# A down projection by seven block products instead of eight, in a two-block transformer kernel

## The chip, the cores and the metric

The kernel runs on one core of a Trainium2 chip. The metric is the device time of one execution in microseconds, taken as the median of several runs. All data are float32, one batch of 1024 tokens with 1024 features.

## The reference, cut to what matters

Two blocks follow each other. The first is attention and a convolutional feed-forward layer, each with a residual and a layer norm:

```
x = layer_norm(ALPHA * x + token_mixer(x), ln1)
u = x @ w_up                       # 1024 -> 2 * 2816
u = causal convolution of width 3 over the tokens, + conv_b
g = value * gelu(gate)             # 1024 tokens x 2816
x = layer_norm(ALPHA * x + g @ w_down, ln2)
```

The second block modulates its activations with six vectors `mod = split(silu(c) @ ada_w + ada_b, 6)`, runs a gated linear attention in two directions (with a context of 256 tokens scanned ahead of the tokens) and a feed-forward layer:

```
a = rmsnorm(x) * (1 + mod[1]) + mod[0]
x = x + mod[2] * gla(a)
h = rmsnorm(x) * (1 + mod[4]) + mod[3]
x = x + mod[5] * (relu(h @ w1) ** 2) @ w2
out = rmsnorm(x)
```

The change concerns `g @ w_down` and the time at which `mod[2]` and `mod[5]` are computed.

## The kernel before, in words

Every float32 operand of a product is split in a high part `h` (cast on ScalarE, L102) and a low part `l` (subtraction on VectorE, L103), and a product is three matmuls, `ah bh + ah bl + al bh` (`mm3`, L130 to L132). A matmul is at most 128 x 128 stationary against 512 moving columns.

The program is written as stages: attention, output projection, first up projection with convolution and gate, first down projection, linear attention, its output projection, second up projection, second down projection. Where stages overlap, `merge` takes generators in turn by the share of a planned cost that each has used. From the order written the framework makes, when it builds the kernel, one fixed order of instructions for each engine: an earlier written instruction goes first among those that are ready by its own estimate of time. A tile takes a free buffer of its tag, and waits if there is none. Loads go out on SyncE's queue (SP), some stores on GpSimd's (POOL), both in order.

The two up projections (`up_pass`) and the second down projection (`mlp_down`) already cut their operands in 2 x 2 blocks and take 7 block products instead of 8, with sums of blocks: left sums S1 to S4, right sums T1 to T4. For the second down projection the left sums are formed in `relu2` and the right ones in `sum_weights`, both stored to device memory and read back as operands.

The first down projection (`ffn_down`) goes a plain way: the gate's result is stored per chunk of 128 hidden features to `g1d` (L1083), and `down_group` takes groups of 2 or 3 chunks, for each group all 8 token tiles and both halves of 512 output columns. `evac` copies (L1111) or adds (L1113) each group's accumulator to `res[t]`; with group 3 it adds the residual, with the last group it forms the layer norm's sum (L585) and calls `layer_norm`. Behind it `norm1(t)` makes the next stage's operands `hi`, `lo`, and `first_values` multiplies them with the first head's value weights. The accumulators have three banks.

Beside the groups run `context` and `modulation`, which calls `ada` for the vectors v = 2 and v = 5, each in four units of 256 columns. A unit loads eight 128 x 256 pieces of `ada_w` (L150), accumulates them on VectorE (L154, L160) in the tile `acc`, of which there is one, and sums over partitions by a matmul (L164). In `ffn_down` the pieces have two buffers of their own (`ar`). The vectors v = 4 and v = 3 are computed in the linear attention, where `ar` is None and the pieces take the four `raw` buffers of `w_get`, through which all weights of that stage pass (L121).

The linear attention writes for each head h: `scan(h)`, then `prepare(h + 1)` (query and key products `fp`, value products `tokp`), then 18 steps of the modulation, which are two units. After the four heads follow the gate products `gate_out` (also `tokp`).

## Time and profile before

| | us |
|---|---|
| median of 3 runs | 2528.82 (2527.7 to 2532.9) |
| profiled execution | 2526.01 |
| its span, first to last instruction | 2524.3 |
| mean granted TensorE clock | 0.992 |

The profile is of one execution. Durations of an engine's groups are unions of its instructions' times, with the mean of one behind them in ns. Matmuls are pipelined, so that the next one starts before the one before it has ended; a stretch of time divided by the matmuls in it gives their spacing. PEclk is the granted TensorE clock as a share of 2.4 GHz.

### The profile page before, as it was taken

How to read it: one execution, taken by the hardware profiler on the slowest of the kernel's cores; microseconds unless marked ns; L12 is line 12 of the kernel's file. 1: busy time of each engine (PE TensorE's matmuls, PEld its weight loads, DVE VectorE, ACT ScalarE, POOL GpSimd, SP SyncE). 2: the span in 40 equal slices, each digit the busy share in tenths (PEclk: the TensorE clock that was granted, in tenths of full speed). 3: DMA queues.
4: the chain of work that ended last, by engine and by line, in shares of the span. 5: the costliest groups of instructions: out<-in, count | busy, mean ns of one | idle time of the engine just before them, and what ended most of it. 6: DMA issues, size and time to landing. Idle time of an engine off the chain costs nothing. (4 is left out here: it accounts for less than half of the span.)

```text
span 2524.3 us, 36732 instructions
## 1 busy us (share of the span) xinstructions
PE 2448.2 (97%) x12954; PEld 2079.2 (82%) x12954; DVE 1707.5 (68%) x3207; ACT 1226.6 (49%) x2208; POOL 416.7 (17%) x655
## 2 busy tenths in 40 slices
PE   8999999998999999899999999999999999999998
PEld 7898989777788888788878798899788888778886
DVE  5776666758777777688658866643588767455456
ACT  5555555734555454653216643332355545544443
POOL 4576641520000000000004000000111111100000
PEclk9999999998999999999999999999999999999999
DMA  5333231253222221465332121211526776566565
GB/s 176 93 92 105 85 87 57 89 186 116 84 76 80 79 90 69 152 195 189 121 119 99 50 71 63 64 61 34 180 94 242 295 272 243 211 234 213 194 209 192
DMA packets 164793, 338.18 MB, mean 134 GB/s; under 512 B 19832, under 2 KB 52216, under 8 KB 164608
## 3 DMA queue, kind: packets, MB, share of 16 engines
q1 hardware_dynamic: 146208, 269.76, 32.8%
q0 software_dynamic: 18400, 66.07, 7.0%
q8 instruction: 102, 1.67, 0.3%
q14 instruction: 83, 0.68, 0.1%
HBM read 247.12 MB, written 80.25 MB: 130 GB/s over the span
## 5 line engine op out<-in xcount | busy, mean ns | idle before, releaser
L130 PE MATMUL s<-act_hi,uh 128*128 128x512 f32 (+1 forms) x640 | 247.2, 386 | 2.0 <-ACT res L774 2.0
L132 PE MATMUL s<-act_hi,ul 128*128 128x512 f32 (+1 forms) x640 | 246.6, 385 | 0.0
L131 PE MATMUL s<-act_lo,uh 128*128 128x512 f32 (+1 forms) x640 | 246.5, 385 | 0.0
L103 DVE TENSOR_TENSOR dpart<-draw,dpart 128x512 fp32r<-128x512 f32 x224 | 146.0, 688 | 124.8 <-ACT dpart L102 123.4
L568 POOL TENSOR_TENSOR rstd<-rstd,mhalf 128x1 f32<-128x1 f32 x74 | 52.6, 713 | 939.8 <-DVE rstd L567 903.2
L102 ACT CAST dpart<-draw 128x512 fp32r<-128x512 f32 x224 | 129.7, 620 | 150.9 <-PE Y L131 66.2
L130 PE MATMUL down<-wdh,gh 128*128 128x512 f32 x352 | 141.6, 403 | 10.9 <-ACT res L1111 5.6
L130 PE MATMUL tokp<-wh,act_hi 128*128 128x256 f32 (+1 forms) x512 | 149.0, 293 | 1.1 <-ACT wh L102 1.1
L132 PE MATMUL tokp<-wh,act_lo 128*128 128x256 f32 (+1 forms) x512 | 148.4, 291 | 1.4 <-DVE act_lo L103 1.4
L131 PE MATMUL tokp<-wl,act_hi 128*128 128x256 f32 (+1 forms) x512 | 149.1, 293 | 0.0
L130 PEld LDWEIGHTS s<-act_hi,uh 128*128 128x128 f32 x640 | 121.7, 190 | 28.4 <-ACT res L774 2.7
L131 PEld LDWEIGHTS s<-act_lo,uh 128*128 128x128 f32 x640 | 121.7, 190 | 25.6
L132 PEld LDWEIGHTS s<-act_hi,ul 128*128 128x128 f32 x640 | 121.5, 190 | 25.8
L131 PE MATMUL down<-wdl,gh 128*128 128x512 f32 x352 | 138.4, 394 | 0.0
L132 PE MATMUL down<-wdh,gl 128*128 128x512 f32 x352 | 136.6, 394 | 0.1
L368 ACT ACTIVATE P<-P,mx 128x640 f32<-128x640 f32 (+7 forms) x128 | 94.4, 738 | 85.7 <-DVE mx L365 79.5
L370 POOL TENSOR_SCALAR P<-P,mx 128x640 f32<-128x640 f32 (+7 forms) x128 | 95.2, 747 | 192.4 <-DVE mx L369 158.5
L130 PE MATMUL s<-ext_8hi,uh 128*128 128x512 f32 (+1 forms) x320 | 123.1, 385 | 0.0
L131 PE MATMUL s<-ext_8lo,uh 128*128 128x512 f32 (+1 forms) x320 | 123.1, 385 | 0.0
L132 PE MATMUL s<-ext_8hi,ul 128*128 128x512 f32 (+1 forms) x320 | 122.9, 384 | 0.0
L103 DVE TENSOR_TENSOR ul<-res,uh 128x1024 fp32r<-128x1024 f32 x80 | 96.6, 1209 | 31.7 <-ACT uh L102 31.3
L102 ACT CAST uh<-s 128x512 fp32r<-128x512 f32 (+1 forms) x72 | 60.3, 837 | 104.8 <-PE s L131 103.2
(364 smaller groups left out, 7275.7 us busy)
## 6 DMA issues: line engine op xcount, KB each, us to landing
ada_w<-in_ada_w SPq DMA_DIRECT2D x192, 128.0 KB, 2.2
res<-in_w_up SPq DMA_DIRECT2D x44, 512.0 KB, 3.4
res<-in_mlp_w SPq DMA_DIRECT2D x32, 512.0 KB, 4.3
draw<-in_mlp_w SPq DMA_DIRECT2D x48, 256.0 KB, 3.4
g1d<-res POOLq DMA_DIRECT2D x22, 512.0 KB, 2.9
gload<-g1d SPq DMA_DIRECT2D x22, 512.0 KB, 4.6
wdraw<-in_w_down SPq DMA_DIRECT2D x44, 256.0 KB, 3.3
raw<-in_wqk SPq DMA_DIRECT2D x32, 256.0 KB, 3.1
```

The source lines that it names most:

```text
L102: ACT.copy(h, raw)
L103: DVE.tensor_tensor(out=l, in0=raw, in1=h, op=ALU.subtract)
L130: PE.matmul(out=o, lhsT=ah, rhs=bh, start=first, stop=False, **kw)
L131: PE.matmul(out=o, lhsT=ah, rhs=bl, start=False, stop=False, **kw)
L132: return PE.matmul(out=o, lhsT=al, rhs=bh, start=False, stop=last, **kw)
L368: ACT.activation(Pm[:, 0:W], Pm[:, 0:W], AF.Exp, bias=mx[:, 0:1], scale=-1.0, accum_out=mx[:, 1:2])
L370: POOL.tensor_scalar(out=Pm[:, 0:W], in0=Pm[:, 0:W], scalar1=mx[:, 2:3], scalar2=0.0, op0=ALU.mult, op1=ALU.add)
L568: POOL.tensor_tensor(out=t[:, 1:2], in0=t[:, 0:1], in1=mhalf, op=ALU.pow)
```

## The change

The first down projection takes 7 block products over all of K: the 22 chunks are 11 pairs (even chunk, odd chunk), tokens and output columns are cut in halves of 512. The right sums (T1 to T4) of `w_down` are formed in the attention by `right_sums` and stored; the left sums are formed in `conv_gate` by `left_sums` for each pair and stored instead of `g1d`. `ffn_down` reads all operands back, product by product, 4 accumulators at a time in five banks; the transposes (`xtp`) share the banks of the context's products. `down_group` is gone. The modulation vectors 2 and 5 are computed in the linear attention, with 36 steps behind each head, in the order 2, 4, 3, 5.

```diff
+    def right_sums(W, n, pl, dst, load, store):
+        w, v = (pl.tile([P, D], F32, tag=x, name=f"sum{x}") for x in "wv")
+        for i, t in enumerate((w, v)):
+            load.dma_start(out=t.rearrange("p (h c) -> p h c", h=2), in_=W[2 * n + i].rearrange("h p c -> p h c"))
+        yield 1
+        DVE.tensor_tensor(out=w[:, XS], in0=w[:, YS], in1=w[:, XS], op=ALU.subtract)
+        DVE.tensor_tensor(out=w[:, YS], in0=v[:, YS], in1=w[:, YS], op=ALU.subtract)
+        yield 1
+        DVE.tensor_tensor(out=v[:, YS], in0=v[:, YS], in1=w[:, XS], op=ALU.subtract)
+        DVE.tensor_tensor(out=v[:, XS], in0=v[:, XS], in1=v[:, YS], op=ALU.subtract)
+        yield 1
+        for x, t in zip(dst, (w, v)):
+            store.dma_start(out=x[n], in_=t)
+    def left_sums(ga, gb, a, b):
+        DVE.tensor_tensor(out=a[:, XS], in0=ga[:, YS], in1=gb[:, YS], op=ALU.add)
+        DVE.tensor_tensor(out=a[:, YS], in0=a[:, XS], in1=ga[:, XS], op=ALU.subtract)
+        DVE.tensor_tensor(out=ga[:, YS], in0=ga[:, XS], in1=ga[:, YS], op=ALU.subtract)
+        DVE.tensor_tensor(out=b, in0=gb[:, XS], in1=a[:, YS], op=ALU.subtract)
...
+        twp = pool(st, "tw", 1)
...
+        def down_sums():
+            for n in range(NCH // 2):
+                yield from right_sums(I["w_down"], n, twp, TW, SP, SP)
+        tws = down_sums()
...
-            merge([(some(mod, 13), 13), (until_pair(), attn_cost(p)), (feed[0], ...), (split_ys(p), 6)])
+            merge([(some(mod, 13), 13), (some(tws, 5), 5), (until_pair(), attn_cost(p)), (feed[0], ...), (split_ys(p), 6)])
...
+        if n % 2 == 0:
+            even[:] = [convc[1].tile([P, T], F32, tag="g", name="geven")]
+            DVE.tensor_tensor(out=even[0], in0=o[0], in1=o[1], op=ALU.mult)
+            return
         DVE.tensor_tensor(out=o[0], in0=o[0], in1=o[1], op=ALU.mult)
-        POOL.dma_start(out=g1d[n], in_=o[0])
+        a, b = convc[1].tile([P, D], F32, tag="s12", name="sums12"), convc[1].tile([P, 512], F32, tag="s4", name="sums4")
+        left_sums(even[0], o[0], a, b)
+        for x, t in (("A12A22", o[0]), ("A11S3", even[0]), ("S1S2", a)):
+            POOL.dma_start(out=left1[x][n // 2], in_=t)
+        POOL.dma_start(out=narrow1["S4"][n // 2], in_=b)
...
+    def block_product(B, raw, left, right, pairs, psums, a, b, by_tile, mm):
+        def operand(name, n, pl, tag):
+            r = raw.tile([P, 512], F32, tag="raw", name="draw")
+            SP.dma_start(out=r, in_=B[name](n))
+            pl = pl()
+            h, l = (pl.tile([P, 512], F32R, tag=tag + x, name="dpart") for x in "hl")
+            split(r, h, l)
+            return h, l
+        def some(t, n, ab):
+            (ah, al), (bh, bl) = ab
+            mm(psums[t], ah[:, toks(t)], al[:, toks(t)], bh, bl, n == 0, n == pairs - 1)
+        ops = {}
+        for n in range(pairs):
+            ops[n] = operand(a, n, left, "s"), operand(b, n, right, "t")
+            if n < pairs - by_tile:
+                for t in range(4):
+                    some(t, n, ops[n])
+                yield
+        for t in range(4):
+            for n in range(pairs - by_tile, pairs):
+                some(t, n, ops[n])
+            yield t
...
-        set_banks(st, "f", {"mm": (1, 3, "down"), "c": (1, 2, "z hps fp tokp"), "ct": (1, 1, "ctp ktp dS"), "tp": (1, 2, "xtp ada")}, ...)
+        set_banks(st, "f", {"mm": (1, 5, "down"), "c": (1, 2, "z hps fp tokp xtp"), "ct": (1, 1, "ctp ktp dS xtp")}, ...)
+        counts = ("r0", 2), ("l0", 2), ("draw1", 4), ("l1", 4), ("r1", 4), ("rp", 2), ("fc1", 1)
...
+        def p1(t, p):
+            ACT.copy(res[t][:, XS], p)
+        def p6(t, p):
+            add(res[t + 4][:, XS], p, res[t][:, XS])
+            with_x1(t, XS, res[t][:, XS])
+        def p2(t, p):
+            complete(t, XS, p)
+        def p5(t, p):
+            add(res[t + 4][:, YS], p, res[t + 4][:, XS])
+            with_x1(t, YS, res[t + 4][:, YS])
+            with_x1(t + 4, YS, res[t + 4][:, YS])
+        def p3(t, p):
+            complete(t, YS, p)
+            with_x1(t + 4, XS, res[t + 4][:, XS])
+            normed(t)
+        def p7(t, p):
+            complete(t + 4, YS, p)
+            add(res[t + 4][:, XS], p, res[t + 4][:, XS])
+        def p4(t, p):
+            complete(t + 4, XS, p)
+            normed(t + 4)
...
+            for a, b, f in (("A11", "B11", p1), ("S2", "T2", p6), ("A12", "B21", p2), ("S1", "T1", p5), ("S4", "B22", p3), ("S3", "T3", p7)):
+                for t in run(a, b, f, 3):
...
-        merge([(most(), 207024), (context(cst), CTXSHARE), (modulation(), 72)])
+        merge([(most(), 179784), (context(cst), CTXSHARE)])
...
-        for t in down_group(groups[last], g1d, Wd, pools, evac(last), True):
-            if t >= 1:
-                norm1(t - 1)
-        norm1(NT - 1)
+        ready = deque(range(4))
+        for t in run("A22", "T4", p4, 3):
+            if ready:
+                norm1(ready.popleft())
+        for t in range(4, NT):
+            norm1(t)
...
     def modulation():
-        for v in (4, 3):
+        for v in (2, 4, 3, 5):
...
-        for _ in range(18):
+        for _ in range(36):
             next(mod, None)
```

`with_x1` loads a piece of the block's input and adds ALPHA times it to an operand; `complete` adds an accumulator and forms the sum of the row; `normed` is `layer_norm` and a store.

## Rows read from the trace of the kernel before

**Rows 1.** The page's first part: busy time, share of the span and instructions of each engine, of the whole execution.

```profile
PE 2448.2 (97%) x12954; PEld 2079.2 (82%) x12954; DVE 1707.5 (68%) x3207; ACT 1226.6 (49%) x2208; POOL 416.7 (17%) x655
```

**Rows 2.** Busy time by stretch. Columns: stretch, its length, busy us of PE, PEld, DVE, ACT and POOL with their instructions, granted clock, DMA share, GB/s. In order: attention; first up projection; first down projection with context; its end; linear attention; second down projection.

```profile
0.00:505.00 505.00, 489.14 (x3189) 433.48 (x3189) 347.45 (x920) 300.63 (x665) 264.14 (x416) 1.00 0.33 98
605.00:1045.00 440.00, 431.09 (x1916) 351.05 (x1915) 328.18 (x359) 219.61 (x274) 12.61 (x23) 0.98 0.22 80
1052.00:1364.00 312.00, 301.13 (x1465) 251.35 (x1466) 229.19 (x449) 121.55 (x230) 22.27 (x23) 0.99 0.49 158
1332.00:1372.00 40.00, 40.00 (x219) 34.26 (x218) 36.04 (x85) 22.42 (x43) 20.57 (x19) 1.00 0.22 81
1410.00:1705.00 295.00, 287.54 (x1807) 259.20 (x1806) 186.54 (x480) 122.01 (x286) 16.94 (x29) 1.00 0.19 61
2202.00:2524.00 322.00, 307.65 (x1347) 253.54 (x1345) 183.96 (x300) 146.95 (x268) 8.42 (x12) 0.98 0.62 207
```

**Rows 3.** Groups of TensorE's instructions, shapes kept apart: line, operation, tiles, shape, count, busy us and mean ns of one, then the idle time before them and what ended it. The first down projection, and two rows of the second.

```profile
L130 PE MATMUL down<-wdh,gh 128*128 128x512 f32 x352 | 141.6, 403 | 10.9 <-ACT res L1111 5.6 <-DVE res L1113 3.3 <-ACT wdh L102 1.2
L130 PE MATMUL X<-dpart 128*128 128x512 f32 x256 | 100.2, 391 | 2.4 <-ACT dpart L102 2.4
L131 PE MATMUL X<-dpart 128*128 128x512 f32 x256 | 100.6, 393 | 1.6 <-DVE dpart L103 1.6
```

**Rows 4.** TensorE alone in a steady stretch of the second down projection: stretch, length, busy us, matmuls that touch it, clock, DMA share, GB/s.

```profile
2260.00:2300.00 40.00, 40.00 (x179) 1.00 0.55 184
```

**Rows 5.** Groups of VectorE's and ScalarE's instructions in 1045 to 1364, columns as in rows 3.

```profile
L1113 DVE TENSOR_TENSOR res<-res,down 128x512 f32<-128x512 f32 x96 | 64.5, 682 | 38.4 <-PE down L132 38.1
L103 DVE TENSOR_TENSOR wdl<-wdraw,wdh 128x512 fp32r<-128x512 f32 x44 | 29.9, 685 | 8.4 <-ACT wdh L102 8.4
L160 DVE SCALAR_TENSOR_TENSOR ada_acc<-ada_w,cs,ada_acc 128x256 f32<-128x256 f32 x56 | 26.8, 479 | 18.3 <-DMA ada_w<-in_ada_w 17.9
L103 DVE TENSOR_TENSOR gl<-gload,gh 128x1024 fp32r<-128x1024 f32 x22 | 26.8, 1220 | 6.1 <-ACT gh L102 6.0
...
L102 ACT CAST wdh<-wdraw 128x512 fp32r<-128x512 f32 x44 | 27.3, 623 | 56.9 <-PE down L132 30.8 <-DMA wdraw<-in_w_down 19.3 <-DVE res L1113 6.5
L102 ACT CAST gh<-gload 128x1024 fp32r<-128x1024 f32 x22 | 22.9, 1051 | 35.1 <-PE down L131 29.2 <-DMA gload<-g1d 5.9
```

**Rows 6.** DMA issues of the whole execution: tiles, queue, count, KB each, median us from issue to landing.

```profile
wdraw<-in_w_down SPq DMA_DIRECT2D x44, 256.0 KB, 3.3
...
draw<-A11S3d SPq DMA_DIRECT2D x32, 256.0 KB, 2.9
```

**Rows 7.** What SyncE's queue waited for, of the whole execution: us in total, times, longest. L1390 is the operand load of the second down projection.

```profile
SPq L1390 <- DVE dpart L103: 176.5, 192, 4.5
```

**Rows 8.** The modulation's wide matmuls, of the whole execution: duration in ns (least, median, most), first and last start, shape.

```profile
L164 PE MATMUL ada<-ada_acc,ones x16: 377/378/382, 1084.2 to 1288.4; 128*128 128x256 f32 x16
```

**Rows 9.** SyncE's queue in order of time in 1440 to 1500 and in 1600 to 1650: start, length of the merged row, line, tiles, count.

```profile
1444.04 21.14 SPq L150 DMA_DIRECT2D ada_w<-in_ada_w  x16
1465.46 2.52 SPq L121 DMA_DIRECT2D raw<-in_g_qk  x4
...
1611.42 30.48 SPq L150 DMA_DIRECT2D ada_w<-in_ada_w  x13
1642.36 7.88 SPq L121 DMA_DIRECT2D raw<-in_g_r  x8
```

**Rows 10.** TensorE in order of time, at seven places: start, length, line, tiles, shape, count, and in brackets the idle time before it and what ended it.

```profile
1263.57 0.65 PE L130 MATMUL down<-wdh,gh 128*128 128x512 f32 x1 [2.38 <-DVE res L1113]
...
1364.36 0.30 PE L130 MATMUL tokp<-wh,act_hi 128*128 128x288 f32 x1
...
1461.71 0.28 PE L175 MATMUL ada<-ones,ada_acc 128*128 128x1 f32 x2
...
1493.27 0.50 PE L175 MATMUL ada<-ones,ada_acc 128*128 128x1 f32 x4
...
1494.33 0.40 PE L130 MATMUL fp<-act_hi,wh 128*128 128x512 f32 x1
...
1638.52 0.50 PE L175 MATMUL ada<-ones,ada_acc 128*128 128x1 f32 x4
...
1644.37 0.54 PE L175 MATMUL ada<-ones,ada_acc 128*128 128x1 f32 x4
1646.06 0.50 PE L130 MATMUL tokp<-wh,act_hi 128*128 128x256 f32 x2 [1.15 <-ACT wh L102]
```

**Rows 11.** TensorE in 1646 to 1714, the matmuls of the tile `o` alone and of the tile `dS` alone: stretch, length, busy us, count, clock, DMA share, GB/s.

```profile
1646.00:1714.00 68.00, 14.16 (x59) 1.00 0.13 40
...
1646.00:1714.00 68.00, 8.32 (x28) 1.00 0.13 40
```

**Rows 12.** Two neighbouring stretches behind the wait of 1263.57, columns as in rows 2.

```profile
1263.80:1267.20 3.40, 3.40 (x9) 2.63 (x9) 1.30 (x3) 0.00 (x0) 0.00 (x0) 0.50 0.86 298
1267.20:1270.60 3.40, 3.40 (x17) 2.77 (x16) 1.78 (x3) 0.00 (x0) 0.00 (x0) 1.00 0.14 48
```

**Rows 13.** One of the sum passes of the second up projection (`relu2`), columns as in rows 3.

```profile
L1344 DVE TENSOR_TENSOR sums<-res,sums 128x512 f32<-128x512 f32 x15 | 10.2, 683 | 0.0
```

136 lines of the change are left out of this document (45 added, 91 removed).

## The prediction, made before the change was run

> **What bounds the kernel now.** I read the page's busy shares first: TensorE 97%, VectorE 68%, ScalarE 49% [rows 1]. Then the busy time by stage: the attention (to 505 us), the first up projection (605 to 1045), the first down projection with the context beside it (1052 to 1364), the linear attention (1410 to 1705) and the last product (from 2202) all keep TensorE over 95% busy, so each matmul taken out of a stage shortens it, and each wait put in lengthens it [rows 2]. VectorE is next: 57% to 75% by stage, 90% at the end of the down projection, 1332 to 1372. Third, the waits inside the down projection: 10.9 us, most of them for accumulators not yet copied out (ScalarE's L1111, VectorE's L1113); the last product, which already works with seven block products, waits 2.4 + 1.6 us in all [rows 3].
>
> **Matmuls removed.** Before: 22 chunks x 8 token tiles x 2 halves x 3 = 1056 matmuls of 512 columns. After: 7 products x 11 pairs x 4 tiles x 3 = 924, so 132 go. Their price isn't their duration: the 391 to 403 ns of a row overlap the next matmul. In a steady stretch of the last product 179 matmuls touch 40 us, two of them begun before it: 40 / 177 = 0.226 us each [rows 4]. 132 x 0.226 = **29.8 us** saved. (By the durations it would be 52 us, which counts the overlap twice.)
>
> **Waits of the down projection.** The eight groups of two or three chunks hand TensorE a new accumulator every 1.4 to 2 us with three banks, and 5.6 + 3.3 us are waits for them [rows 3]. After, a product has four accumulators for some 30 us and a fifth bank; only its last three pairs are done tile by tile, 9 matmuls or 2.0 us apart, and a copy takes 0.6 to 0.7 us [rows 5]. I take the waits of the last product, 4.0 us, for the 10.9: **-6.9**; ends 0 and -10.9.
>
> **Operands of the down projection.** Splits before: 22 of 1024 columns and 44 of 512. After: 154 of 512. ScalarE: 154 x 0.623 = 96 us for 50; VectorE: 154 x 0.685 = 105 us for 57, but 64.5 us of L1113 become about 44 passes of 0.69, 30 us, and 27 us of modulation leave [rows 5]. VectorE's 229 of 312 us [rows 2] hardly moves. Loads: 154 x 256 KB = 40 MB for 23, less 8.4 MB of modulation. Four landing buffers turn: 2.9 us from issue to landing [rows 6], 0.62 cast, 0.69 subtraction, some 0.6 of queueing: 4.8 us, 1.2 us an operand. The stage shrinks to about 312 - 42 = 270 us, 1.75 us an operand. So TensorE stays the pace, as in the last product, where the load queue waits 176.5 us for buffers to come free [rows 7] at 1.44 us an operand. Cost nothing; if each turn took 8 us instead (rival 4), the cover would be gone.
>
> **Modulation moved.** Eight units (v = 2 and 5) of eight 128 KB loads, eight VectorE passes and one wide matmul go from the down projection to the linear attention. TensorE's part (16 instructions of at most 0.38 us [rows 8]) is the same in both places: 0. In the down projection they had two load buffers of their own; in the linear attention they share the four `raw` buffers with the weights that TensorE needs. The SyncE rows show the queue: 16 modulation loads take 1444 to 1465, and only behind them come the four loads of the next head's query and key weights (1465.5); at the end the gate weights come at 1642.4, behind the last modulation load [rows 9]. A unit also holds the one accumulator tile until its own small matmul, which TensorE does late: the second unit's at 1493.3, one us ahead of the next head's first product (1494.3). The last two units stand 1638.5 and 1644.4, so a unit takes 5.85 us when TensorE lets it through, and the gate product starts 1.7 us behind [rows 10]. Now four units per head stand there instead of two. Head 0: two more behind 1493.3: 1493.3 + 11.7 + 1.7 = 1506.7, 12.4 us late. Head 1: one of its units can be done between query/key and value products, so one exposed: 6.5 us. Heads 2 and 3 have no weights to load between them but the gate's: four more units, 23.4 us late. Sum 42.3 us. Queued behind: every weight load, then TensorE. What fills it are the scans, which need no weights: in 1646 to 1714 TensorE has 14.2 + 8.3 us of them for `o` and `dS` alone [rows 11], and they are a chain of VectorE and ScalarE, which the 27 us of added VectorE work slows. No row shows how fast a scan runs alone; lower end 0 idle (all filled), upper 42.3 (none). I take two thirds filled, **+15**, nearer the lower, since scan work of about 22 us a head lies beside each delay.
>
> **The clock.** After the 2.38 us wait that ended at 1263.57 [rows 10] the granted clock is 0.50, the 1.2 GHz level, and 9 matmuls touch 3.4 us where the next 3.4 us, at 1.00, hold 17: 8 lost, 1.8 us [rows 12]. The down projection has two such falls, both behind accumulator waits; I take one for the new one, and two in the linear attention: **+1.7**. The Trainium skill (TensorE: Matmul & The Clock Gate, Part 1: The HAM clock gate) says that half rate is the default and activity lifts it; the trace agrees (0.50 behind the 2.38 us wait). By that rule each of the three delays in the linear attention brings a fall, and the sum would be 1.8 us more.
>
> **Sums.** Weight sums: 11 x 4 passes of 0.683 us [rows 13], 30 us of VectorE in the attention, where it is busy 347 of 505 us, and 23 MB more through SyncE. The loads of a pair wait for the stores of the pair before (one buffer each), and bias and weight loads queue behind them. No row shows that: from 0 to a quarter of the passes, 7.5; I take **+2**, since TensorE waits 16 us in the whole stage and part of that is the start. Product sums: 30 us in the up projection, VectorE from 328 to 358 of 440 us (81%), from 0 to 7.5: **+1.5**. The stores, 1.75 MB a pair for 1 MB, go out through GpSimd, busy 13 us there: 0.
>
> **The end of the stage.** Before, eight tiles are normed in the last group; after, four are normed under the last product and four behind it. 36 us of VectorE in 1332 to 1372 for about six tiles [rows 2] is 6 us a tile, 24 us for four, begun 6 us before the product ends; TensorE has 25 us of value products meanwhile. Cost 0 (rival 5 otherwise).
>
> **Sum.** The profiled execution took 2526.0 us: 2526.0 - 29.8 - 6.9 + 15 + 1.7 + 2 + 1.5 = 2509.5. The median of the three runs is 2.8 above the profiled one; some of that I keep: **2511**.
>
> **Rivals.** (1) *Forecast*: as above, 2500 to 2522; chance 0.45. (2) *The modulation hides*: the order of instructions lets units through earlier and scans fill the rest. For it: at 1461.7 a unit's matmul went in the midst of value products; against: the second waited to 1493.3. No idle, no falls there: 2511 - 15 - 3.6 = 2492; 0.25. (3) *The modulation starves the linear attention*: scans don't fill and the whole 42.3 us stand, with one fall more: 2511 + 27.3 + 1.8 = 2540, slower. It decides from about 32 us of idle on, where 29.8 + 6.9 less 5.2 is used up. Against: 22 us of scan work per head; 0.10. (4) *Loads pace the new down projection*, the change failing of its aim: a turn of 8 us makes 154 x 2.0 = 308 us for 270: 2549; TensorE binds up to 1.75 us an operand, each 0.1 beyond costs 15. Against: the last product's 1.44; for: there it has six landing buffers and no context; 0.07. (5) *Banks shared at the end*: the transposes of the norm now use the banks of the value products. If these are handed out in the order written, value products, which start at 1364.36, right behind the last matmul of the stage, while later tiles are still transposed [rows 10], must wait for the seventh tile, about 12 us behind the product's end, with 5 us of transposes in it: +7, 2518; 0.13.
>
> **Range and chances.** 3 and 4 lie above 2530 and hold 0.17; so the range is 2490 to 2527, from the case of no idle to the forecast's with most of it. Within 0.2% of 2528.8 (2523.7 to 2533.9), about what this measurement tells from no change, lie the top of 1 and 5 and a little of 3 and 4: 0.07. Faster 0.80, slower 0.13. With most on one side, the likeliest case's own range is 2500 to 2522.
>
> **What would show it.** In the profile after: 924 matmuls of the down product at a spacing of 0.226; its waits near 4 us, none for an evacuation over 1 us; the stage near 270 us. In the linear attention: 128 modulation loads, the next heads' query and key weights 10 us and 6 us later after the value products than now, a gate product some 20 us later against its scan, TensorE's idle up from 7.5 to some 20 us in that stage, and one or two stretches of clock 0.50. Attention and up projection longer by 1 to 3 us each. I am wrong if the linear attention has no more idle than now (then 2), if it stands for all of its delay (3), if the down projection waits for ScalarE's or VectorE's halves of operands all along it (4), or if value products begin 7 us or more after the last down matmul (5).

## The result and the profile after

The changed kernel takes **2559.8 us** (median of 4 runs, 2552.8 to 2560.5) where the kernel before takes 2529.0 in the same comparison: 1.0113 of it, 95% interval 1.0092 to 1.0134. It is slower; forecast was 2511, with a range to 2527. The profiled execution took 2559.2 us, its span is 2557.5.

The page's first part, as in [rows 1], now of the changed kernel:

```profile
PE 2425.3 (95%) x12822; PEld 2066.3 (81%) x12822; DVE 1744.9 (68%) x3299; ACT 1260.3 (49%) x2284; POOL 445.6 (17%) x677
```

TensorE has its 132 matmuls less and is busy 23 us less, in a span that is 33 us longer: it stands still more. Where, the next table tells. A stage begins with its first matmul; "to the last gate product" begins with the last matmul of the down projection and holds the value products and the linear attention. Us, from the trace of one execution each. The same code scatters from trace to trace: the attention is the same in the changed kernel, e1, e2, e4, e7, e13 and e15 to e18, and takes 523.4 to 528.1 there; the down projection without the modulation takes 283.3 to 290.4, the second up pass with the changed kernel's code 312.8 to 319.8, and the stretch to the last gate product 415.2 to 419.8 in e7, e9, e12 and e18. So a difference of less than some 5 us between two rows means little.

| kernel | attention | first up pass | down projection | to the last gate product | second up pass |
|---|---|---|---|---|---|
| before | 505.4 | 441.6 | 311.4 | 396.0 | 320.9 |
| changed | 525.7 | 430.6 | 287.0 | 446.2 | 315.2 |
| e1 modulation back | 523.4 | 430.6 | 299.9 | 411.0 | 314.9 |
| e2 own load buffers | 524.0 | 430.7 | 283.3 | 419.9 | 317.4 |
| e3 late sums | 528.1 | 430.0 | 286.5 | 447.9 | 317.7 |
| e4 values between norms | 524.5 | 432.0 | 287.0 | 445.9 | 315.5 |
| e5 before, moved 128 bytes | 506.4 | 432.3 | 310.9 | 396.2 | 318.5 |
| e6 sums, transfers only | 513.5 | 431.4 | 285.9 | 445.2 | 315.7 |
| e7 = e2 + own banks | 527.4 | 431.9 | 283.6 | 416.5 | 312.8 |
| e8 sums in up pass | 506.6 | 466.6 | 283.7 | 446.8 | 314.4 |
| e9 = e7, sums on GpSimd in up pass | 507.0 | 465.0 | 287.3 | 419.8 | 315.3 |
| e10 = e9 + modulation on GpSimd | 504.7 | 463.1 | 290.4 | 436.0 | 316.5 |
| e11 = e10 + aligned weights | 513.1 | 462.8 | 289.9 | 430.6 | 315.8 |
| e12 = e7 + paced sums | 532.9 | 429.4 | 287.1 | 415.2 | 317.7 |
| e13 = e7, no passes | 528.1 | 430.8 | 288.4 | 419.0 | 316.5 |
| e14 = e1 + own banks, paced sums | 536.9 | 431.7 | 304.3 | 403.2 | 316.9 |
| e15 = e7, one load | 523.4 | 429.5 | 285.5 | 409.6 | 316.3 |
| e16 = e7, no matmul | 523.9 | 431.9 | 285.6 | 410.7 | 319.8 |
| e17 stores on GpSimd's queue | 524.0 | 433.2 | 286.3 | 446.1 | 317.6 |
| e18 = e7 + e17 | 524.4 | 431.0 | 283.7 | 416.5 | 316.7 |

So the attention loses 20.3, the down projection gains 24.4, the linear attention with the stage's end loses 50.2, and, unforeseen, the two up passes gain 11.0 and 5.7 (the second of these lies within the scatter); with 2.8 lost in the output projection the sum is +32, against 33.2 between the spans.

**The down projection.** TensorE's groups in 1060 to 1356, columns as in [rows 3]:

```profile
L131 PE MATMUL down<-dpart 128*128 128x512 f32 x308 | 121.7, 396 | 0.4 <-DVE dpart L103 0.2
L132 PE MATMUL down<-dpart 128*128 128x512 f32 x308 | 120.9, 393 | 0.0
L130 PE MATMUL down<-dpart 128*128 128x512 f32 x308 | 117.7, 395 | 2.2 <-ACT dpart L102 2.2
```

924 matmuls, and 2.6 us of waits for 10.9 [rows 3]: that part did as forecast. But TensorE's waits in 1065 to 1351 have a new head, the context that runs beside it:

```profile
PE ctp L91 <- ACT ctx_x L943: 4.8, 2, 3.1
PE ctp L91 <- ACT ctx_f L639: 4.2, 1, 4.2
```

Us in all, times, longest. In the kernel before, no wait for the context's norm is among TensorE's in this stage; here it is 9.0 us. Why it was hidden before, no run tells. It is at the stage's start that TensorE stands more, and the granted clock is lower there too. The first 60 us of the stage, changed and before (columns as in [rows 2]):

```profile
1066.00:1126.00 60.00, 49.29 (x219) 39.25 (x219) 38.04 (x59) 39.72 (x77) 6.83 (x10) 0.89 0.82 267
```

```profile
1053.00:1113.00 60.00, 54.41 (x259) 44.62 (x258) 47.94 (x81) 42.69 (x82) 4.76 (x7) 0.97 0.78 265
```

**The end of the stage.** TensorE in order of time; the last down product, the four late norms, the first value product:

```profile
1351.86 0.39 PE L132 MATMUL down<-dpart 128*128 128x512 f32 x1
1363.87 4.46 PE L693 MATMUL xtp<-diag,res 128*128 128x128 f32 x24 [11.62 <-DVE rstd L600]
...
1374.10 0.38 PE L130 MATMUL tokp<-wh,act_hi 128*128 128x288 f32 x1
```

The number in brackets is the engine's idle time before the instruction, and what ended it: 11.6 us of standstill, and the first value product 22.2 us behind the last down product; before it came 0.3 us behind [rows 10]. Of the clock: in 1363.9 to 1367.3, right behind the wait, the granted clock is 0.55, then 1.00.

```profile
1363.90:1367.30 3.40, 3.40 (x17) 3.40 (x18) 3.40 (x5) 1.26 (x3) 2.30 (x3) 0.55 0.21 83
1367.30:1370.70 3.40, 2.05 (x18) 1.86 (x18) 2.62 (x7) 3.40 (x10) 2.00 (x2) 1.00 0.58 228
```

**The linear attention.** SyncE's queue, columns as in [rows 9]: behind the units that are written after head 0, where head 2's weights come next, and the gate weights:

```profile
1465.57 0.85 SPq L150 DMA_DIRECT2D ada_w<-in_ada_w  x2
1491.95 0.33 SPq L169 DMA_DIRECT2D m2d<-ada_o  x1
...
1504.64 3.51 SPq L121 DMA_DIRECT2D raw<-in_g_qk  x4
...
1699.94 4.79 SPq L121 DMA_DIRECT2D raw<-in_g_r  x5
```

For 26 us, 1466 to 1492, nothing leaves, because the queue's head, the store of a unit, waits for VectorE's work on a unit, as SyncE's waits in 1455 to 1495 show (us in all, times, longest):

```profile
SPq L169 <- DVE ada_acc L154: 26.2, 2, 25.7
```

Head 2's weights go out at 1504.6, before at 1465.5 [rows 9]; the gate's at 1699.9, before at 1642.4. TensorE shows what they wait for: units of modulation that come to their matmul only at 1490.7 and later, head 2's first product right behind the last:

```profile
1490.66 0.59 PE L164 MATMUL ada<-ada_acc,ones 128*128 128x256 f32 x2
1498.89 0.59 PE L164 MATMUL ada<-ada_acc,ones 128*128 128x256 f32 x2
1507.91 0.64 PE L164 MATMUL ada<-ada_acc,ones 128*128 128x256 f32 x2
1508.79 0.50 PE L130 MATMUL fp<-act_hi,wh 128*128 128x512 f32 x1
...
1703.23 1.22 PE L164 MATMUL ada<-ada_acc,ones 128*128 128x256 f32 x2 [3.00 <-DVE ada_acc L160]
1703.89 0.99 PE L130 MATMUL tokp<-wh,act_hi 128*128 128x256 f32 x2
```

Then all 768 gate matmuls stand in one block without a break, while the last scan ran alone before them. The same 58 us in the changed kernel and before (columns as in [rows 2]):

```profile
1646.00:1704.00 58.00, 40.46 (x197) 30.43 (x196) 37.64 (x106) 14.47 (x40) 5.87 (x10) 0.89 0.41 126
```

```profile
1646.00:1704.00 58.00, 57.94 (x427) 55.77 (x427) 24.92 (x64) 20.46 (x53) 4.72 (x8) 1.00 0.14 46
```

### The profile page after: what moved, and what is told of

It reads as the page before. It is cut to its first block, busy times and chain, and to the rows that moved or that the text cites. A ratio compares the mean times of both kernels' runs of the same rounds, so it can differ in the third digit from the quotient of the medians.

```text
span 2557.5 us, 37112 instructions
## 1 busy us (share of the span) xinstructions
PE 2425.3 (95%) x12822; PEld 2066.3 (81%) x12822; DVE 1744.9 (68%) x3299; ACT 1260.3 (49%) x2284; POOL 445.6 (17%) x677
## 5 line engine op out<-in xcount | busy, mean ns | idle before, releaser
L103 DVE TENSOR_TENSOR dpart<-draw,dpart 128x512 fp32r<-128x512 f32 x378 | 250.6, 693 | 183.2 <-ACT dpart L102 175.9
L102 ACT CAST dpart<-draw 128x512 fp32r<-128x512 f32 x378 | 221.5, 620 | 243.5 <-PE Y L131 65.7
L131 PEld LDWEIGHTS s<-act_lo,uh 128*128 128x128 f32 x640 | 121.7, 190 | 22.2
L131 PE MATMUL down<-dpart 128*128 128x512 f32 x308 | 121.7, 396 | 0.4 <-DVE dpart L103 0.2
L132 PE MATMUL down<-dpart 128*128 128x512 f32 x308 | 120.9, 393 | 0.0
L102 ACT CAST uh<-res 128x1024 fp32r<-128x1024 f32 x80 | 83.0, 1040 | 77.0 <-PE s L131 61.4
L130 PE MATMUL down<-dpart 128*128 128x512 f32 x308 | 117.7, 395 | 2.2 <-ACT dpart L102 2.2
```

What stands on the lines that cost most here:

```text
L102: ACT.copy(h, raw)
L103: DVE.tensor_tensor(out=l, in0=raw, in1=h, op=ALU.subtract)
L130: PE.matmul(out=o, lhsT=ah, rhs=bh, start=first, stop=False, **kw)
L131: PE.matmul(out=o, lhsT=ah, rhs=bl, start=False, stop=False, **kw)
L132: return PE.matmul(out=o, lhsT=al, rhs=bh, start=False, stop=last, **kw)
```

## The experiments

The diffs show only the lines that matter; a remark behind `#` in them isn't in the kernel. Ratios are to the kernel before, with a 95% interval behind them.

### What starves the linear attention

**e1**: the modulation back beside the down projection.

```diff
+        merge([(most(), 179784), (context(cst), CTXSHARE), (modulation(), 72)])   # v = 2, 5; own ar (2), ac (1); "ada" on bank "c"
-        for _ in range(36):
+        for _ in range(18):                                                       # linear attention: v = 4, 3
```

> The changed kernel, with the modulation v = 2 and 5 put back beside the down projection (two load buffers of its own, 8 units there; 18 steps per head in the linear attention). Theory (the moved modulation starves the linear attention of weights, rival 3 of the prediction): the stretch from the last matmul of the down projection to the last gate product, 446 us in the changed kernel and 396 before, falls to 396 plus the 11.6 us stall at its start, about 408; the down projection, 287 us, grows by 0 to 5; the kernel takes about 2560 - 38 + 3 = 2525 us, ratio to before 0.998. Counter-theory (the linear attention is slow for another reason, the banks or the late norms at its start): that stretch stays above 435 us and the kernel above 2545. Second counter-theory (the modulation cost as much where it stood): the down projection grows by 20 us or more.

Measured: 1.0028 of before (1.0013 to 1.0043). The stretch to the last gate product falls to 411.0, 35 us less; the down projection pays 12.9. So the moved modulation costs the linear attention 35, where the prediction had 15. The theory holds there, but not in its time for the kernel, 2525 us (2535.3 measured): the bill at the old place I had put at 0 to 5.

**e2**: own load buffers.

```diff
+    ac, ar = pool(gla_st, "ac", 1), pool(gla_st, "ar", 4)
-                yield from ada(v, c, 256, None, ac)
+                yield from ada(v, c, 256, ar, ac)
```

> The changed kernel, with the modulation left in the linear attention but its loads given four buffers of their own there instead of the four that the weights use; nothing else. Theory (the harm is that the weights' loads queue behind modulation loads for the same buffers): the stretch from the end of the down projection to the last gate product falls from 446 to 410 - 420 us, the gate products begin within 10 us of their place before the change, the kernel takes 2525 to 2535 us. Rival (the chain of scan, VectorE and the single accumulator tile holds the units, the buffers are only where it shows): the stretch stays above 435, the kernel above 2548, since loads in SyncE's queue still wait in order for units that have not been summed.

Measured: 0.9998 (0.9985 to 1.0010): some 30 us gone by one line, 26 of them in this stretch. The gate weights start early:

```profile
1613.81 0.33 SPq L121 DMA_DIRECT2D raw<-in_g_r  x1
```

and in the 58 us shown above TensorE is busy throughout:

```profile
1646.00:1704.00 58.00, 58.00 (x441) 56.15 (x441) 39.97 (x102) 20.09 (x47) 3.49 (x5) 1.00 0.45 135
```

**e17**, **e18**: the eight stores of these units on another queue, without and with own buffers and banks. They test another reading of the queue: that the store at its head (L169 above) blocks it.

```diff
-            SP.dma_start(out=(m2d if v == 2 else m5d)[:, cols], in_=o)
+            POOL.dma_start(out=(m2d if v == 2 else m5d)[:, cols], in_=o)
```

> The changed kernel (2559.8 us), with the eight stores of the moved modulation units (m2d, m5d) issued from GpSimd's queue instead of SyncE's; buffers stay shared. In the changed kernel SyncE stands 25.7 us (1466 to 1492) before such a store, which waits for its unit's matmul, with the next head's weight loads behind it. Theory A (the store at the head of SyncE's queue is what starves the products): the stretch from the last down product to the last gate product falls from 446 to 420 - 428 us, as with own load buffers, the kernel to 2532 - 2542. Theory B (the shared buffers starve them; the store only stands where the wait shows): it stays above 438, the kernel above 2550.

Measured: 1.0114 (1.0087 to 1.0142), stretch 446.1. The wait only moved on to the next load, as SyncE's waits in 1400 to 1710 show:

```profile
SPq L150 <- DVE ada_acc L154: 51.9, 14, 24.9
```

> The same move of the eight stores in the kernel with own load buffers and own banks (2523.9 us; stretch 416.5). Theory (the 7 us that went with the units' matmuls were waits of SyncE behind stores that wait for them): the stretch comes to 407 - 411 us, the kernel to 2514 - 2519. Rival (the matmuls cost by their place between scans and products, and by the gates' bank): it stays above 414, the kernel above 2521.

Measured: 0.9972 (0.9962 to 0.9983), stretch 416.5 as without the move. The stores are innocent at both places; the shared buffers starved the products.

**e13, e15, e16**: what the rest, 416.5 for 396.0, is made of. From e7 (below): seven of the eight passes of each unit v = 2, 5 left out; seven of eight loads and passes left out; the matmul left out.

```diff
-                else:
+                elif v not in (2, 5):                           # e13: no passes behind the first
-        for k in range(KD):
+        for k in range(1 if v in (2, 5) else KD):               # e15: one load, one pass
-            PE.matmul(out=psum, lhsT=ones.to_broadcast([P, P]), rhs=accs[0], start=True, stop=True)
-            DVE.tensor_tensor(out=o, in0=o, in1=psum, op=ALU.add)
+            DVE.tensor_tensor(out=o, in0=o, in1=accs[0], op=ALU.add)   # e16
```

> The kernel with own load buffers and own banks, where in the linear attention seven of the eight VectorE passes of each unit of v = 2 and 5 are left out (56 passes, 24 us); the loads, the matmuls and the stores stay, so the two modulation rows are wrong. It tells what holds the linear attention at 416.5 us, with 396 before, when it has buffers of its own. Theory (VectorE's passes, in the midst of its chain of states): the stretch from the last down product to the last gate product falls to 394 - 402 us. Rival (the transfers, or the unit's matmuls and their accumulator tile in the written order): it stays above 411.

> The kernel with own load buffers and own banks (stretch from the last down product to the last gate product 416.5 us), where in the linear attention each unit of v = 2 and 5 makes one of its eight loads and one of its eight passes; matmuls, sums with the bias and stores stay, so the two modulation rows are wrong. Without seven of the passes, but with all loads, the stretch was 419.0. Theory (the 56 loads of 128 KB delay the loads of the weights on SyncE): it falls to 400 - 406 us, as with the modulation beside the down projection (403.2). Rival (the units' matmuls, which take a bank of the gates and stand between scans and products in the written order, hold it): it stays above 412.

> The kernel with own load buffers and own banks, where the units of v = 2 and 5 make all loads and passes but not their matmul: the sum over the partitions is left out, so the two modulation rows are wrong, and the bank of the gates is not taken for them. Theory of the loads: the stretch stays above 412 us. Rival (the matmuls and their bank): it falls to 400 - 406. If both runs of this pair fall halfway, loads and matmuls share the cost; if neither falls, the order in which products and scans are issued has changed for another reason.

Measured: 419.0, 409.6, 410.7. VectorE's passes cost nothing: that theory fell. Loads and matmuls give back 6 to 7 us each, where 13 (to e14's 403.2) were looked for: they seem to share it. These are single executions, the same code scatters by 4.6 us, and even e14, without this modulation in the stretch, stays 7 above 396.0: that part isn't the modulation's. e18 excludes that the matmul's share is a wait of its store.

### The end of the down projection

**e4**: value products written between the late norms.

```diff
         for t in range(4, NT):
+            next(values)
             norm1(t)
```

> The changed kernel, with the value products of tiles 0 to 3 written between the norms of tiles 4 to 7 at the end of the down projection, instead of all behind them; the same work. Theory (shared banks are handed out in the order written, so value products stood behind the transposes of tile 7: rival 5 of the prediction): the 11.6 us in which TensorE stands still behind the last down product fall under 3 us, value products begin within 3 us of it, and the kernel takes 2548 to 2553 us. Rival (the value weights or VectorE's queue are not ready then anyway): the stall stays above 8 us and the kernel within 4 us of 2560.

Measured: 1.0114 (1.0096 to 1.0131), nothing won. The first value product comes at once, and TensorE waits behind it instead:

```profile
1358.22 0.40 PE L91 MATMUL hps<-ident,res 128*32 128x128 f32 x1 [4.34 <-DVE res L1203]
1362.40 3.78 PE L693 MATMUL xtp<-diag,res 128*128 128x128 f32 x16 [3.79 <-DVE rstd L600]
```

**e7**: e2, and the value products in the five banks of the down products.

```diff
+        banks["tokp"] = banks["down"]
         values = first_values()
```

> The kernel with own load buffers for the modulation (2527.6 us), and at the end of the down projection the value products take the five banks of the down products instead of sharing two with the transposes; the written order stays. Theory (the 11.6 us stall comes from shared banks alone, and with the modulation no longer starving the linear attention nothing else waits at its end): value products begin under 3 us behind the last down product, the stretch from there to the last gate product falls from 420 to 406 - 412, the kernel takes 2514 to 2520 us. Rival (as the run with values between the norms suggests, the time comes back behind it: norms and scans on VectorE set the pace): the stall goes and the stretch stays above 414, the kernel above 2523.

Measured: 0.9977 (0.9966 to 0.9988), faster than before by an interval that excludes 1. The written order is unchanged and the standstill gone, so it was the banks. But of 11.6 us only 3.4 arrive: the rest returns at the start of the linear attention, as waits for VectorE, which has the late norms to do first:

```profile
1403.87 1.22 PE L863 MATMUL z<-hs,a2s 96*128 96x512 f32 x2 [3.54 <-DVE hs L853]
1407.64 0.80 PE L863 MATMUL z<-hs,a2s 96*128 96x512 f32 x1 [2.55 <-DVE t L868]
```

### The weight sums in the attention

**e3**: the sums written from the fourth pair of heads on.

```diff
-            merge([(some(mod, 13), 13), (some(tws, 5), 5), ...
+            merge([(some(mod, 13), 13), (some(tws if p >= 3 else iter(()), 7), 7), ...
```

> The changed kernel, with the weight sums of the attention begun with the fourth pair of heads (seven steps per pair) instead of the first (five); the same work. Theory (the 20 us that the attention lost come from the sums being crowded into its first 180 us, where the transfers are already dense): the first matmul of the output projection, at 525.7 us in the changed kernel and 505.4 before, comes at 507 to 512; the kernel takes 2560 - 15 = about 2545 us. Rival (30 us of VectorE passes cost the attention TensorE time wherever they stand): it stays at 520 to 528, with the waits moved to later pairs; the kernel stays within 5 us of 2560.

Measured: 1.0122 (1.0106 to 1.0138), attention 528.1. The run tested nothing: the sums depend on nothing, so the order in which the program is laid out does not follow where they are written; the loads stand at the same places of SyncE's queue. 32 to 182, columns as in [rows 2], in order before, changed, e3:

```profile
32.00:182.00 150.00, 148.02 (x1017) 136.44 (x1018) 105.91 (x284) 83.20 (x202) 98.29 (x165) 0.99 0.32 89
```

```profile
32.00:182.00 150.00, 137.13 (x847) 121.25 (x848) 114.43 (x287) 74.63 (x178) 97.36 (x146) 0.95 0.68 222
```

```profile
32.00:182.00 150.00, 136.44 (x823) 118.52 (x822) 113.24 (x279) 70.35 (x170) 93.63 (x135) 0.94 0.69 221
```

The attention loses its time here: 847 instructions of TensorE for 1017, with a DMA share of 0.68 for 0.32 and a clock of 0.95.

**e12**: e7 with the sums really spread, by an order on SyncE's queue.

```diff
-                SP.dma_start(out=o[to, c].bitcast(F32), in_=i[of, c].bitcast(F32))
+                mark[:] = [SP.dma_start(out=o[to, c].bitcast(F32), in_=i[of, c].bitcast(F32))]
+            with tc.issue_after(mark[0].ins):      # in right_sums, around each load
```

> The kernel with own load buffers and own banks (2523.9 us), with the loads of each weight sum in the attention queued on SyncE behind the latest of the transfers that finish a pair's keys, so that the eleven sums are really spread over the pairs of heads; the run with late sums did not spread them: its loads stand at the same places of SyncE's queue as in the changed kernel, in the first 180 us, wherever the code names them. Theory (the attention's 20 us come from the crowd in its first 180 us, where transfers and VectorE are already dense): the first matmul of the output projection comes at 508 to 515 us for 527, the kernel takes 2506 to 2515 us. Rival (44 passes of 0.69 us cost the same wherever they stand, 12 us for the passes and 8 for the transfers): it stays at 523 or later, the kernel at 2518 or more.

Measured: 1.0023 (1.0011 to 1.0035), attention 532.9. The first part improves, and the loss is then found behind it:

```profile
32.00:182.00 150.00, 143.15 (x929) 129.31 (x930) 108.65 (x287) 79.79 (x190) 95.80 (x156) 0.97 0.50 154
182.00:482.00 300.00, 292.33 (x1878) 259.65 (x1877) 201.89 (x539) 159.06 (x355) 133.93 (x204) 0.97 0.38 119
```

In the changed kernel TensorE is busy 299.2 of the latter 300 us. So crowding alone is not the cause: spread over the stage (their loads now run from 39 to 404 us) the sums cost no less, 27.5 us here, and 31.5 in e14, whose attention has the same code. The order that spreads them also holds back what stands behind them on SyncE's queue; whether some of the cost is that was not tried apart.

**e6**: the transfers without the passes.

```diff
-        DVE.tensor_tensor(out=w[:, XS], in0=w[:, YS], in1=w[:, XS], op=ALU.subtract)   # and the three others of right_sums
```

> The changed kernel without the 44 VectorE passes of the weight sums in the attention: the blocks of w_down are loaded and stored again unsummed, so the products that use T1 to T4 get wrong operands. Theory A, the rival of the late sums that the last runs left standing (the passes of VectorE hold TensorE's S banks, wherever they stand): the first matmul of the output projection, 525.7 us in the changed kernel, comes at 505 to 509. Theory B (the 46 MB of loads and stores, and the loads queued behind them, cost the time): it stays at 520 or later. In between, both, in proportion.

Measured: attention 513.5 (one execution), between the two theories: of the 20 us about 8 stay with the transfers (23 MB, not the 46 of the expectation), and about 12 go with the passes. The split is rough, since the scatter is nearly 5 us, and without passes the stores also leave earlier. Three of the four kinds of pass are longer here, 816 to 835 ns, than in the second up pass, 683 [rows 13]; the fourth takes 680. Two groups of the changed kernel's attention:

```profile
L197 DVE TENSOR_TENSOR sumw<-sumv,sumw 128x512 f32<-128x512 f32 x11 | 9.2, 835 | 10.7 <-DMA sumv<-in_w_down 10.5
L199 DVE TENSOR_TENSOR sumv<-sumv,sumw 128x512 f32<-128x512 f32 x11 | 9.0, 820 | 0.1
```

TensorE meets VectorE's load at the softmax: it waits for the pass that adds the biases to a tile of scores and takes their extremes (`mx`), before it may write the next tile. Us in all, times, longest in 32 to 505, before, and in the whole of the changed kernel:

```profile
PE S L360 <- DVE mx L365: 0.7, 1, 0.7
```

```profile
PE S L386 <- DVE mx L391: 8.0, 9, 1.4
```

**e8, e9**: the sums in the first up pass, on VectorE and (from e7) on GpSimd.

```diff
         POOL.dma_start(out=narrow1["S4"][n // 2], in_=b)
+        drain(right_sums(I["w_down"], n // 2, convc[2], TW, SP, SP))     # e9: passes on POOL, stores in POOL's queue
```

> The changed kernel with the weight sums moved out of the attention into the first up pass, one pair of chunks behind every second chunk (its pool for product sums holds one buffer for that, not two). Theory (the sums cost the attention its 20 us; in the up pass eight accumulators leave VectorE room): the attention returns to 505 - 508 us; the up pass, 430.6 us with VectorE busy 347 of 430, grows by 0 to 6 us; the kernel takes 2540 to 2548. Rival (VectorE becomes the bound of the up pass, 377 of 430 us with the evacuations late): the up pass grows by 15 us or more and the kernel stays at 2555 or above.

> The kernel with own load buffers and own banks (2523.9 us), with the weight sums in the first up pass instead of the attention, their 44 passes on GpSimd instead of VectorE, and their stores in GpSimd's queue. GpSimd is busy 21 of the 430 us there; its subtraction of 512 columns takes 1.30 us in the attention, so 44 of them 57 us. Theory (in the up pass with sums on VectorE the 36 us came from VectorE alone): the attention takes 506 to 508 us as without sums, the up pass 430 to 434, the kernel 2502 to 2507 us. Rival (the transfers of the sums, queued before the loads of the up pass, or GpSimd's work slowing VectorE beside it, cost the up pass): it takes 445 us or more, the kernel 2515 or more.

Measured: 1.0146 (1.0127 to 1.0164) and 1.0082 (1.0067 to 1.0097). The attention is whole again (506.6, 507.0), so the sums are all that it lost; the up pass pays 36 and 34, and both rivals held. In e8 TensorE's main wait in 640 to 1060 is for accumulators that ScalarE has yet to copy out (20.1 us in e9; the largest there in the changed kernel is 3.9):

```profile
PE s L130 <- ACT res L793: 23.4, 5, 6.8
```

On GpSimd a pass takes 1.5 to 1.9 us instead of 1.30, and VectorE's own work grows beside it; the same pass of the up pass in the changed kernel and in e9:

```profile
L1064 DVE SCALAR_TENSOR_TENSOR res<-res,convc,res 128x1022 f32<-128x1022 f32 x42 | 53.7, 1279 | 0.6
```

```profile
L1057 DVE SCALAR_TENSOR_TENSOR res<-res,convc,res 128x1022 f32<-128x1022 f32 x40 | 56.1, 1401 | 0.6
L199 POOL TENSOR_TENSOR sumv<-sumv,sumw 128x512 f32<-128x512 f32 x9 | 16.7, 1853 | 0.6
```

Both kernels also hold one buffer of product sums instead of two, which was not tried apart. VectorE has no wait for such a buffer in 640 to 1060, so nothing shows that it costs; but how much of the 36 and 34 it is, stays open.

**e10**: the modulation on GpSimd too.

```diff
-                elif v < 2:
+                elif v < 2 or ar:        # a product and a sum on POOL instead of one pass on DVE
```

> The same, with all 128 multiply-add passes of the modulation in the linear attention done on GpSimd (a product of 0.57 us and a sum of 0.78 us each, as in the attention, 173 us of its time there, where it is busy 20 of 398) instead of VectorE (54 us of its time). Theory (with buffers and banks of its own the linear attention is held by VectorE, whose chain of states the added 27 us lengthen): the stretch from the last down product to the last gate product, 416.5 us, falls to 390 - 402, and the kernel by 14 to 25 us. Rival (the stretch is held by the written order of scans and products, or by the transfers): it stays above 410. Second rival (the reciprocal roots that GpSimd makes for the scans now wait behind the modulation): above 420.

Measured: 1.0149 (1.0132 to 1.0166); the stretch grows from 419.8 to 436.0. e11, with the same code there, has 430.6, so the growth is 11 to 16 us. That is the second rival's number without its mechanism: VectorE's waits for GpSimd's roots only go from 10.9 to 15.9 us. VectorE has 34 us less to do there and is slower at what is left, and the granted clock in 1400 to 1800 is 0.94 for 0.97; e9, then e10, 1400 to 1800:

```profile
L867 DVE TENSOR_TENSOR_SCAN t<-ones,t 128x128 f32<-128x128 f32 x64 | 22.1, 405 | 0.1
L1249 DVE SCALAR_TENSOR_TENSOR eq<-fp,eq 128x512 f32<-128x512 f32 x16 | 10.8, 681 | 0.0
```

```profile
L867 DVE TENSOR_TENSOR_SCAN t<-ones,t 128x128 f32<-128x128 f32 x64 | 29.3, 514 | 0.1
L1249 DVE SCALAR_TENSOR_TENSOR eq<-fp,eq 128x512 f32<-128x512 f32 x16 | 10.8, 679 | 0.2 <-ACT eq L877 0.2
```

### Why the up passes became faster

**e5**: the kernel before with one unused tile.

```diff
+    apart = resp.tile([P, 32], F32, name="apart")
+    POOL.memset(apart, 0.0)
     small = pool(ctx, "small", 4)
```

> The kernel before, with one unused tile of 128 bytes per partition put in front of the pool `small`, so that every tile of the stages behind the attention that lies on the left side of SBUF moves up by 128 bytes; no other difference. Seen so far: in both up passes and in the two square products the 512-column matmuls come every 227 ns in the changed kernel and every 233 ns before, though their code is the same; the changed kernel has lost a small buffer of 4 x 32 bytes, and so their weights begin at an address that is 224 modulo 256, as their moving operand does, and before at 96. Theory (the distance between the addresses of weights and moving operand sets the spacing): spacing 227 here too; the first up pass, 441.6 us before, takes about 430, the second, 320.9, about 315, the square products and feature products 2 to 5 us less; the kernel takes 2506 to 2513 us, 0.992 to 0.994 of before. Rival (the spacing comes from what the change does beside the matmuls: sums, stores, order): spacing 233, kernel within 4 us of 2529.

Measured: 0.9958 (0.9943 to 0.9973), about 11 us for 128 bytes. TensorE in 700 to 1000, in order before, changed, e5:

```profile
700.00:1000.00 300.00, 300.00 (x1289) 1.00 0.22 79
```

```profile
700.00:1000.00 300.00, 300.00 (x1325) 1.00 0.29 102
```

```profile
700.00:1000.00 300.00, 299.50 (x1318) 1.00 0.23 81
```

300 us over 1289 is 233 ns, over 1325 is 226; median spacing 232, 227 and 227. The kernel won less than the 16 to 23 us looked for: the second up pass came down by 2.4, not 5.7. So some 11 us of the changed kernel's time are no merit of the change: against the moved kernel before, 2521.2 us, it is 1.0113 / 0.9958 = 1.0156, 39 us slower, and e7 and e18 (2523.9, 2523.7), which beat the kernel before, are not faster than that one.

**e11**: the weights' tiles of the attention 2304 bytes apart.

```diff
+            s = 576 if m == 528 else m
-            r = rawp.tile([P, m], F32, tag="raw", name="raw")
+            r = rawp.tile([P, s], F32, tag="raw", name="raw")[:, 0:m]      # wh and wl alike
```

> The same again, with the weight tiles of the attention allocated 2304 bytes apart instead of 2112, so that all of them, not one in four, begin at 224 modulo 256, as their moving operand does. Theory (the spacing goes by the distance of the addresses): the projections of 512 columns come every 227 ns instead of 232 to 233, some 700 of them, and the attention is 3 to 5 us shorter. Rival (the moving operand and its addresses are not what tells the two apart there, since other work lies between): spacing and stage stay within 1 us.

Measured: 1.0131 (1.0115 to 1.0146). Where the projections' matmuls follow each other directly, their mean spacing goes from 232.2 to 230.6 ns only, though 227 becomes the commonest, and the attention is longer, 513.1 for 504.7. Inconclusive: other work lies between these matmuls, and I can't say what made the stage longer.

### The parts together

**e14**: e1, with the banks of e7 and the paced sums of e12.

```diff
+        merge([(most(), 179784), (context(cst), CTXSHARE), (modulation(), 72)])
+        banks["tokp"] = banks["down"]
+            with tc.issue_after(mark[0].ins):
```

> The changed kernel with the modulation of v = 2 and 5 beside the down projection again, the value products in the banks of the down products, and the paced weight sums. By the runs so far: the down projection 297 to 300 us (287 without the modulation), the stretch to the last gate product 395 to 402 us, the attention as in the run with paced sums. Theory (the modulation costs less beside the seven products, 13 us, than in the linear attention, 20 us): 4 to 10 us below the kernel with paced sums and the modulation in the linear attention, so about 2503 us; rival (the two places cost the same): within 3 us of it.

Measured: 1.0034 (1.0022 to 1.0046), 2539.3 us, within 3 us of e12's 2536.6: the theory fell and the rival held. The modulation costs about the same at either place (304.3 and 403.2 for 287.1 and 415.2), once it has buffers of its own.

## Why the prediction was wrong, point by point

- **Matmuls removed, -29.8.** Right: a steady stream of them comes at 227 ns in both kernels, and 132 x 0.227 is 30.0 us.
- **Accumulator waits, -6.9.** Right for these waits (10.9 to 2.6), wrong for the stage: 9.0 us of waits for the context's norm took their place at its start. The stage is 287.0 us, where these two terms alone would make 311.4 - 36.7 = 275. What is left is about the context's waits and the clock: in the trace 13.7 us of the stage stand at 0.50, 6.8 before.
- **Operands at no cost.** Right; rival 4 is refuted: 2.6 us of waits for operands in the whole stage.
- **Modulation moved, +15 and +1.7.** The step that failed: the price of an added unit, and how much of the delay the scans fill. The mechanism was right, units held the weights back and the weights TensorE. Counted from the last down product, head 0's first feature product comes 7.5 us later than before; that much of the standstill at the stage's end arrives there. From there head 2's first one (1508.8, before 1494.3 [rows 10]) is 19.2 us later for 12.4 forecast, head 3's 4.4 more for 6.5, and the first gate product 39.0 more for 23.4: 62.6 us for the 42.3 that I had put as the upper end. I had priced an added unit at 5.85 us. The matmuls of the three units at 1490.7 to 1507.9 come 8.2 and 9.0 us apart, and the stores of the last four 8 to 11 (1676.6, 1685.7, 1696.6 and 1704.9). The scans filled some 20 us, by which the block of gate products became shorter (94.2 us, before 114.0), not two thirds: 62.6 - 19.9 + 7.5 = 50.2, as the table has it. Without this modulation the stretch is 35 us shorter (e1), for 15 forecast. This is rival 3, at more than its price; own buffers (e2) give back 26 of the 35, and what loads and matmuls hold is 6 to 7 us each at most. The clock's +1.7 was too small as well: in 1374 to 1798 the granted clock is 0.97, 24 us of it at 0.50, and in 1364 to 1760 before it is 1.00.
- **The end of the stage, 0.** Failed: rival 5 happened too, 11.6 us of standstill. Its cause was named rightly (e7), its price not: without it VectorE's norms make the next products wait, so only about 3 us were to be had.
- **Attention, +2.** Failed by ten times: 20.3. The step that took VectorE's 347 of 505 us for room was wrong: the softmax goes through VectorE between two matmuls, and TensorE's waits for its pass over the scores go from 0.7 to 8.0 us. That a pass delays TensorE wherever it stands fits e12 but isn't shown. Of the two terms, a quarter of the passes, 7.5, was too low for about 12, and the transfers, put at nothing, cost about 8 (e6).
- **Up projection, +1.5.** Nothing of it is seen, under an unforeseen gain of 11.0 from addresses: e5, at the same addresses but without the product sums, takes 432.3 us there, the changed kernel 430.6.
- **The sum.** -24.4, +50.2, +20.3, -16.7, +2.8 against -16.5 forecast. Rivals 3 and 5 and the bound of the attention were written as alternatives; all three came. The miss would have been some 11 us larger without the gain from addresses, which was luck.

## What to carry to other kernels

Work moved into another stage costs there what its buffers, banks and queue places cost, not what its engines' busy shares leave free: give moved work its own buffers before judging it (one line was worth about 30 us). Where a scheduler lays out the order, an experiment that only writes work elsewhere may change nothing; look at the queue before believing it. And compare kernels at equal addresses: 128 bytes of an unrelated buffer were worth as much as a third of the matmuls saved.

## What the runs showed of the hardware

- **Spacing of matmuls by address.** A stream of 512-column matmuls comes every 227 ns where weights and moving operand begin at the same address modulo 256, and every 233 where they lie 128 apart. In the compiled programs, weights and moving operand of the up passes begin at 96 and 224 (before), 224 and 224 (changed, e5); those of the last product at 96 and 96 (before) and 224 and 224 (changed), with 227 both times; and products of the linear attention at 96 and 224 (before), with 232, and 224 and 224 (changed), with 227. So it is the distance, not the place. e5 shows it by moving 128 bytes and nothing else. The experiments made from the changed kernel keep its distances, but for e11's attention, so this is no part of their differences; e11, with distances mixed, leaves open how far it holds under other work.
- **GpSimd slows VectorE, but only some of it.** With GpSimd busy 172 of 410 us (28 in e9), VectorE's scan over two SBUF tiles goes from 405 to 514 ns, and its product with a PSUM input stays (681, 679). Single instructions of e10 show that it is the overlap: four scans in a row take 1.37 us at 1432.8, where GpSimd is idle, and 2.73 at 1645.6, where it is busy 2.65 us of them, while five of the PSUM products run beside GpSimd and take 0.66 to 0.68. The Trainium skill (SBUF — State Buffer, Who interferes with whom) says that a VectorE instruction with two SBUF inputs contends with a GpSimd instruction that reads SBUF, and that one with at most one SBUF input does not, outside VectorE's modes that use both of its ports; both rows agree. Not every such instruction is slowed: of eight subtractions of two SBUF tiles in e10 (L874) one runs beside GpSimd, and takes 0.68 us like the others. It would also fit the three kinds of pass of 0.82 us in the attention, where GpSimd is busy half the time, for 0.68 in the second up pass, but no run shows that it is the cause.
